# Right forms in quarter-size pieces, and pairs of two kinds in alternation, in the up-projection of a gated MLP

## The chip, the cores and the metric

The kernel runs on one core of a Trainium2 chip. The core has TensorE (PE, matrix products; its weight loads are listed as PEld), VectorE (DVE), ScalarE (ACT), GpSimd (POOL) and SyncE (SP, which here only issues DMAs). Each engine works through its own list of instructions in order, and engines wait for each other through semaphores. The metric is the device time of one execution in microseconds (us).

## The reference

One layer of a decoder trunk on a sequence of 1024 positions and 1024 channels: a block of three mixers, a cross-attention, and a gated MLP. The change lies in the gated MLP:

```
def conv_gated_ffn(h, w_up, conv_w, conv_b, w_down):
    u, v = jnp.split(h @ w_up, 2, axis=-1)
    u = causal depthwise convolution of width 3 (u, conv_w) + conv_b
    return (jax.nn.silu(u) * v) @ w_down
```

The block is cut here to its core. `h @ w_up` is 1024x1024 by 1024x5632, so u and v have 2816 channels each, which are 22 blocks of 128 (`NFF` = 22).

## The kernel before

`ffn_up` computes `h @ w_up` as 22 pairs. Pair f is the u block f and the v block 22 + f, 128 channels each, over all 1024 positions. The two halves of the positions and the two halves of the inner dimension make it a 2x2x2 block product, and it is done with seven products in place of eight (a Winograd form). Each product is a left form (made of weights) by a right form (made of activations).

A product (`prod`, L1292 to 1297) is 12 matmuls of 128x128 by 128x512: four steps of the inner dimension, and three for each, since every form is split into a rounded part `hi` and a rest `lo`, and hi·hi, hi·lo and lo·hi are summed. It needs the `lo` of its left form from the second or third matmul on, not at the first.

**Left forms** (`left`, L1263 to 1290). GpSimd makes the sums S1 to S4 of the weight blocks (L1280), ScalarE casts the hi part (L1287), and VectorE or GpSimd subtracts it for the lo part (L1288). In the kernel before, the forms take turns: one on VectorE, the next on GpSimd. A form lies in a tile `wf` from a pool with two tags of two buffers each, so a fifth form has to wait until TensorE has finished with the first.

**Right forms** (`right`, L1299 to 1319) are built once. From the transposed activations in four tiles `h3r` (128x2048) it makes T1 to T4 and takes B22 as it is; each is then split in hi (ScalarE, L1306) and lo (L1307; VectorE for T1 to T3, GpSimd for T4 and B22). Every step is one instruction of 128x2048.

**Work ahead** (`ahead`). While the activations are still being made and while the right forms are built, TensorE does the products A11·X0 and A12·X1 of pairs 0 to 7 (they need plain activations only), and the results go to DRAM (`part`) by way of `s1` (after the first product) and `c11` (L1353, after both, out of the bank `ps_a`). So pairs 0 to 7 have five products left, T2, T3, T1, T4, B22 in the code's order, and pairs 8 to 21 have seven, with A11 and A12. In the following they are called fives and sevens. A five holds 60 matmuls, a seven 84.

**A pair** (`pair`, L1355 to 1395) sums its products in PSUM: `ps_b2` for T2 (pool mps), `ps_cd` with two halves for T3+T4 and T1+B22 (pool dps, two buffers), `ps_a` for A11+A12. VectorE reads them out into u2, u3, vt and u (L1377 to 1388), and when u is complete the convolution and the gate follow: ScalarE L1390, VectorE L1391 and L1392, ScalarE's silu L1393, GpSimd's multiplication y·vt L1394 (128x1024), and a DMA to DRAM. The weights of the next pair are loaded when a pair is begun.

The pairs run in the order 0 to 21: eight fives, then fourteen sevens. `ffn_down` follows and reads y from DRAM (`acr`), splits it into `ap` (L1444, L1445) and multiplies (L1431, tile `ps_dn`).

Each engine's order of instructions is not the order of the code: a scheduler that simulates the program sets it when the kernel is built, so that products of neighbouring pairs are interleaved. A change of sizes or of the loop's order moves instructions on all engines.

Of the kernel before, what the change touches and what calls it, by code (L numbers as in the profile page):

```python
# [12 lines left out]
F32 = mybir.dt.float32  # L13
# [4 lines left out]
ALU = mybir.AluOpType  # L18
# [9 lines left out]
NFF = 22  # L28
# [68 lines left out]
class K:  # L97
# [1169 lines left out]
    def left(self, r1, r2, which, sp):  # L1267

        nc = self.nc
        V, A, G = nc.vector, nc.scalar, nc.gpsimd  # L1270
        q = {f"A{n}{k + 1}": r[:, 4 * k:4 * k + 4, :] for n, r in ((1, r1), (2, r2)) if r is not None for k in range(2)}
        sums = {"S1": ("A21", "A22", ALU.add), "S2": ("S1", "A11", ALU.subtract), "S3": ("A11", "A21", ALU.subtract),
                "S4": ("A12", "S2", ALU.subtract)}

        def get(n):
            if n not in q:
                a, b, op = sums[n]
                a, b = get(a), get(b)
                q[n] = b if n == "S4" else sp.tile([P, 4, P], F32, tag=n, name=n)
                G.tensor_tensor(out=q[n], in0=a, in1=b, op=op)  # L1280
            return q[n]

        for n in which:
            x = get(n)
            self.nform = getattr(self, "nform", 0) + 1
            f = self.wp.tile([P, 2, 4, P], F32R, tag=("whi", "wlo")[self.nform % 2], name="wf")
            A.copy(out=f[:, 0], in_=x)  # L1287
            (V if self.nform % 2 else G).tensor_tensor(out=f[:, 1], in0=x, in1=f[:, 0].bitcast(F32), op=ALU.subtract)  # L1288
            yield f

    def prod(self, ps, f, x, start, stop):
# [7 lines left out]
    def right(self, X, raw):  # L1299

        nc = self.nc
        V, A, G = nc.vector, nc.scalar, nc.gpsimd

        def parts(x, nm, eng):
            f = [self.quad(f"{nm}{p}") for p in ("hi", "lo")]
            A.copy(out=f[0], in_=x)  # L1306
            eng.tensor_tensor(out=f[1], in0=x, in1=f[0].bitcast(F32), op=ALU.subtract)  # L1307
            return f
        b11, b21, b12, b22 = raw[0, 0], raw[1, 0], raw[0, 1], raw[1, 1]
        V.tensor_tensor(out=b11, in0=b12, in1=b11, op=ALU.subtract)  # L1310
        t2 = self.quad("t2r", F32)
        V.tensor_tensor(out=t2, in0=b22, in1=b11, op=ALU.subtract)
        G.tensor_tensor(out=b12, in0=b22, in1=b12, op=ALU.subtract)
        X["T2"] = parts(t2, "T2", V)
        X["T3"] = parts(b12, "T3", V)
        G.tensor_tensor(out=b21, in0=b21, in1=t2, op=ALU.subtract)
        X["T1"] = parts(b11, "T1", V)
        X["T4"] = parts(b21, "T4", G)
        X["B22"] = parts(b22, "B22", G)

    def ffn_up(self, X, raw, act, part, spill):

        nc, tc, I = self.nc, self.tc, self.I
        V, A, G, T = nc.vector, nc.scalar, nc.gpsimd, nc.tensor
        with tc.tile_pool(name="up", bufs=1) as sp:
            col = lambda j, f: self.pc("ffn_conv_w", NFF * j + f) if j < 3 else self.pc("ffn_conv_b", f)
            nraw = itertools.count()
            ne = part.shape[1]

            def load(m):  # L1330
                n = next(nraw) % 6
                r = self.wp.tile([P, NK, P], F32, tag="raw", name="raw") if n < 2 else \
                    self.res.tile([P, NK, P], F32, tag=f"r{n}", name="raw")
                nc.sync.dma_start(out=r, in_=I["t_up"][m])
                return r
# [10 lines left out]
            def ahead(f):  # L1346
                forms, a = self.left(load(f), None, ("A11", "A12"), sp), bank(f)
                self.prod(a, next(forms), X[0], True, True)
                nc.sync.dma_start(out=part[0, f], in_=copy("s1", a))
                yield  # L1350
                self.prod(a, next(forms), X[1], False, True)
                c = spill.tile([P, 512], F32, tag="acr", name="c11")
                A.copy(out=c, in_=a)  # L1353
                nc.sync.dma_start(out=part[1, f], in_=c)
                yield  # L1355
# [42 lines left out]
            for f in range(ne):  # L1398
                g = ahead(f)
# [3 lines left out]
                prev = g  # L1403
            next(prev)
            self.right(X, raw)
            rs = [load(0), load(NFF)]
            for f in range(NFF):
                nx = [load(f + 1), load(NFF + f + 1)] if f + 1 < NFF else None
                pair(f, rs)
                rs = nx  # L1410

# [133 lines left out]
```

## Time and profile of the kernel before

| what | value |
|---|---|
| median of 3 runs | 2471.76 us (2469.12 to 2471.86) |
| the profiled execution | 2471.44 us, of which the trace spans 2469.7 us |
| TensorE busy | 2361.9 us, 96% of the span, 15224 matmuls |
| VectorE, ScalarE, GpSimd busy | 1256.0 us (51%), 884.7 us (36%), 758.3 us (31%) |
| mean granted clock of TensorE | 0.987 of full speed |
| ffn_up from the right forms to the end | about 1757 to 2228 us of the span |

Times within the trace are microseconds from the span's start. In a row of the timeline, the number in square brackets at its end is the idle time of the engine before this instruction and what ended it. A matmul's row shows 0.39 us, but the next one may start 0.23 us after it began, since matmuls overlap.

### The profile page before, as it was taken

How to read it: one execution, taken by the hardware profiler on the slowest of the kernel's cores; microseconds unless marked ns; L12 is line 12 of the kernel's file. 1: busy time of each engine (PE TensorE's matmuls, PEld its weight loads, DVE VectorE, ACT ScalarE, POOL GpSimd, SP SyncE). 2: the span in 40 equal slices, each digit the busy share in tenths (PEclk: the TensorE clock that was granted, in tenths of full speed). 3: DMA queues.
4: the chain of work that ended last, by engine and by line, in shares of the span. 5: the costliest groups of instructions: out<-in, count | busy, mean ns of one | idle time of the engine just before them, and what ended most of it. 6: DMA issues, size and time to landing. Idle time of an engine off the chain costs nothing. (4 is left out here: it accounts for less than half of the span.)

```text
span 2469.7 us, 37037 instructions
## 1 busy us (share of the span) xinstructions
PE 2361.9 (96%) x15224; PEld 1968.0 (80%) x15224; DVE 1256.0 (51%) x1964; ACT 884.7 (36%) x1359; POOL 758.3 (31%) x613
## 2 busy tenths in 40 slices
PE   7999999999999999999999999999898999999998
PEld 7987768686777887878787789999776777777887
DVE  6446465657336447463653554544645544466322
ACT  6543222231215335353541222433433333344321
POOL 1011011110112314233321620430577666764210
PEclk9999999999999999999999999999999999999999
DMA  8644213121222111111114541224453222237431
GB/s 301 233 153 128 82 57 95 57 95 40 95 68 68 59 46 35 52 43 52 43 65 166 180 162 35 94 77 138 132 174 130 91 80 77 77 113 272 158 135 47
DMA packets 100329, 259.45 MB, mean 105 GB/s; under 512 B 26048, under 2 KB 30784, under 8 KB 100160
## 3 DMA queue, kind: packets, MB, share of 16 engines
q1 hardware_dynamic: 98720, 253.01, 31.2%
q0 software_dynamic: 1008, 3.67, 0.5%
q8 instruction: 119, 1.95, 0.3%
q14 instruction: 50, 0.41, 0.0%
q10 hardware_dynamic: 432, 0.41, 0.0%
HBM read 195.19 MB, written 61.87 MB: 104 GB/s over the span
## 5 line engine op out<-in xcount | busy, mean ns | idle before, releaser
L155 PE MATMUL ps_d<-hThi,whi 128*128 128x512 f32 x1056 | 426.1, 404 | 2.1 <-DVE Ktt L261 1.7
L157 PE MATMUL ps_d<-hTlo,whi 128*128 128x512 f32 x1056 | 424.8, 403 | 0.0
L159 PE MATMUL ps_d<-hThi,wlo 128*128 128x512 f32 x1056 | 423.9, 402 | 0.0
L140 ACT CAST whi<-raw 128x1024 fp32r<-128x1024 f32 (+1 forms) x162 | 158.5, 985 | 339.3 <-PE ps_d L157 171.0
L1431 PE MATMUL ps_dn<-wd,ap 128*128 128x512 f32 x1056 | 242.3, 391 | 5.3 <-ACT ap L1444 3.0
L1431 PEld LDWEIGHTS ps_dn<-wd,ap 128*128 128x128 f32 x1056 | 199.1, 189 | 48.4 <-ACT ap L1444 3.9
L155 PEld LDWEIGHTS ps_d<-hThi,whi 128*128 128x128 f32 x1056 | 199.8, 189 | 44.7 <-issue 3.2
L157 PEld LDWEIGHTS ps_d<-hTlo,whi 128*128 128x128 f32 x1056 | 199.9, 189 | 43.0 <-issue 4.8
L159 PEld LDWEIGHTS ps_d<-hThi,wlo 128*128 128x128 f32 x1056 | 199.7, 189 | 42.7 <-issue 4.2
L143 POOL TENSOR_TENSOR wlo<-raw,whi 128x1024 fp32r<-128x1024 f32 (+1 forms) x45 | 96.0, 2133 | 446.1 <-ACT whi L140 353.9
L143 DVE TENSOR_TENSOR wlo<-raw,whi 128x1024 fp32r<-128x1024 f32 (+1 forms) x117 | 147.7, 1271 | 95.0 <-ACT whi L140 94.9
L1295 PE MATMUL ps_a<-h3hi,wf 128*128 128x512 f32 x352 | 118.0, 402 | 8.7 <-DVE wf L1288 6.7
L1287 ACT CAST wf<-S 128x512 fp32r<-128x512 f32 x88 | 54.7, 622 | 143.4 <-PE ps_cd L1295 96.9
L1445 DVE TENSOR_TENSOR ap<-acr,ap 128x512 fp32r<-128x512 f32 x44 | 44.2, 1006 | 114.6 <-ACT ap L1444 114.6
L1109 POOL TENSOR_SCALAR ms<-ms 128x1 f32<-128x1 f32 x33 | 8.3, 251 | 287.4 <-ACT xn L1108 178.4
L1295 PEld LDWEIGHTS ps_a<-h3hi,wf 128*128 128x128 f32 x352 | 67.6, 193 | 27.7 <-DVE wf L1288 8.0
L1442 POOL TENSOR_TENSOR wd<-wdr,wd 128x1024 fp32r<-128x1024 f32 x22 | 56.5, 2569 | 93.4 <-ACT wd L1441 84.9
L155 PE MATMUL ps_d<-ohi,whi 128*128 128x512 f32 x192 | 75.7, 398 | 7.2 <-ACT ohi L1160 7.2
L745 DVE CUSTOM_DVE_ANT_0 a_p<-ps_s,a_bias 128x512 f32<-128x512 f32 (+3 forms) x96 | 51.8, 553 | 52.4 <-PE ps_s L743 46.9
L1094 PE MATMUL ps_tm<-whi,h2Thi 128*128 128x256 f32 x256 | 75.3, 294 | 1.7 <-ACT s_p L1222 1.7
L755 ACT ACTIVATE a_p<-a_p,a_nm 128x128 f32<-128x128 f32 (+7 forms) x64 | 49.2, 769 | 76.4 <-POOL a_nm L751 59.5
L157 PE MATMUL ps_d<-olo,whi 128*128 128x512 f32 x192 | 76.1, 396 | 0.3 <-DVE olo L1161 0.3
(411 smaller groups left out, 5680.8 us busy)
## 6 DMA issues: line engine op xcount, KB each, us to landing
raw<-t_in SPq DMA_DIRECT2D x66, 512.0 KB, 3.8
raw<-t_up SPq DMA_DIRECT2D x52, 512.0 KB, 3.7
wdr<-ffn_w_down SPq DMA_DIRECT2D x44, 512.0 KB, 4.3
th_dram<-th SPq DMA_DIRECT2D x24, 512.0 KB, 2.8
mth<-th_dram SPq DMA_DIRECT2D x24, 512.0 KB, 3.7
acr<-act_dram SPq DMA_DIRECT2D x44, 256.0 KB, 2.7
act_dram<-y SPq DMA_DIRECT2D x20, 512.0 KB, 2.6
raw<-t_kv SPq DMA_DIRECT2D x16, 512.0 KB, 5.0
```

The lines of the kernel that those rows point to most:

```text
L140: nc.scalar.copy(out=hi, in_=raw)
L143: eng.tensor_tensor(out=lo, in0=raw, in1=hi.bitcast(F32), op=ALU.subtract)
L155: nc.tensor.matmul(o, lhsT=hi[:, k, :], rhs=xhi(k, h), start=(k == 0), stop=False)
L157: nc.tensor.matmul(o, lhsT=hi[:, k, :], rhs=xlo(k, h), start=False, stop=False)
L159: nc.tensor.matmul(o, lhsT=lo[:, k, :], rhs=xhi(k, h), start=False, stop=(k == nk - 1))
L745: V.tensor_tensor_reduce(out=p_[:, a:b], in0=ps[:, 0:b - a], in1=bias[:, 1024 - n + a:1024 - n + b], op0=ALU.add, op1=ALU.max, scale=1.0, ...
L755: A.activation(out=pr[c][:, 0:n], in_=pr[c][:, 0:n], func=AF.Exp, bias=nm[:, c:c + 1], accum_out=Z[:, c:c + 1])
L1094: nc.tensor.matmul(o, lhsT=xh, rhs=hi[:, k % 4, :], start=(k == 0), stop=False)
L1287: A.copy(out=f[:, 0], in_=x)
L1295: self.nc.tensor.matmul(ps, lhsT=f[:, a, k, :], rhs=x[b][:, k, :], start=(start and n == 0), stop=(stop and n == 11), skip_group_check=not ...
L1431: T.matmul(ps[j][c], lhsT=a[:, p, P * j:P * j + P], rhs=w[q][:, 512 * c:512 * c + 512], start=(f == 0 and n == 0), stop=(f == NFF - 1 and ...
L1442: (V if f % 2 else G).tensor_tensor(out=w[:, 1], in0=wr, in1=w[:, 0].bitcast(F32), op=ALU.subtract)
```

## The change

Three edits. In `right`, every instruction of 128x2048 becomes four of 128x512, one for each step k of the inner dimension; cast and lo alternate within a form in the code. In `left`, the lo parts go two to VectorE and one to GpSimd in turn, where they went one and one. In `ffn_up`, the loop takes the pairs in the order 0, 8, 1, 9, ... 7, 15, 16, ... 21: a five and a seven alternate eight times, then six sevens.

```
-            (V if self.nform % 2 else G).tensor_tensor(out=f[:, 1], in0=x, in1=f[:, 0].bitcast(F32), op=ALU.subtract)
+            (V if self.nform % 3 else G).tensor_tensor(out=f[:, 1], in0=x, in1=f[:, 0].bitcast(F32), op=ALU.subtract)
...
+        def sub(eng, out, in0, in1):
+            for k in range(4):
+                eng.tensor_tensor(out=out[:, k, :], in0=in0[:, k, :], in1=in1[:, k, :], op=ALU.subtract)
+
         def parts(x, nm, eng):
             f = [self.quad(f"{nm}{p}") for p in ("hi", "lo")]
-            A.copy(out=f[0], in_=x)
-            eng.tensor_tensor(out=f[1], in0=x, in1=f[0].bitcast(F32), op=ALU.subtract)
+            for k in range(4):
+                A.copy(out=f[0][:, k, :], in_=x[:, k, :])
+                eng.tensor_tensor(out=f[1][:, k, :], in0=x[:, k, :], in1=f[0][:, k, :].bitcast(F32), op=ALU.subtract)
             return f
...
-        V.tensor_tensor(out=b11, in0=b12, in1=b11, op=ALU.subtract)
+        sub(V, b11, b12, b11)
...
-        G.tensor_tensor(out=b21, in0=b21, in1=t2, op=ALU.subtract)
+        sub(G, b21, b21, t2)
...
+            order = [f for g in range(ne) for f in (g, ne + g)] + list(range(2 * ne, NFF))
             rs = [load(0), load(NFF)]
-            for f in range(NFF):
-                nx = [load(f + 1), load(NFF + f + 1)] if f + 1 < NFF else None
+            for n, f in enumerate(order):
+                nx = [load(order[n + 1]), load(NFF + order[n + 1])] if n + 1 < NFF else None
                 pair(f, rs)
                 rs = nx
```

The lines after these move down: the read-outs of a pair stand at L1382 to L1393 in the changed kernel, the matmul of `ffn_down` at L1437. The `sub` of the right forms is at L1306, the cast at L1311 and the lo at L1312.

Where the instructions stand is shown at three places. The first is the building of the right forms, on VectorE. `h3r00` is b11 in the code, `h3r01` is b12, and `wf_15720` is the left form A12 of one of the pairs that are done ahead; TensorE needs it next after `wf_15741`. Before:

```order
L1310 TENSOR_TENSOR h3r00_14875<-h3r01_15439,h3r00_14875 128x2048
L1312 TENSOR_TENSOR t2r_15913<-h3r11_15446,h3r00_14875 128x2048
L1307 TENSOR_TENSOR T2lo_15917<-t2r_15913,T2hi_15916 128x2048
L1307 TENSOR_TENSOR T3lo_15921<-h3r01_15439,T3hi_15920 128x2048
L1288 TENSOR_TENSOR wf_15720<-raw_15660,wf_15720 128x512
L1307 TENSOR_TENSOR T1lo_15926<-h3r00_14875,T1hi_15925 128x2048
L1288 TENSOR_TENSOR wf_15759<-raw_15699,wf_15759 128x512
```

and now:

```order
L1306 TENSOR_TENSOR h3r00_14875<-h3r01_15439,h3r00_14875 128x512 x4
L1306 TENSOR_TENSOR t2r_15916<-h3r11_15446,h3r00_14875 128x512 x4
L1288 TENSOR_TENSOR wf_15741<-raw_15738,wf_15741 128x512
L1312 TENSOR_TENSOR T2lo_15926<-t2r_15916,T2hi_15925 128x512 x4
L1312 TENSOR_TENSOR T3lo_15936<-h3r01_15439,T3hi_15935 128x512 x4
L1312 TENSOR_TENSOR T1lo_15950<-h3r00_14875,T1hi_15949 128x512 x4
L1288 TENSOR_TENSOR wf_15720<-raw_15660,wf_15720 128x512
L1288 TENSOR_TENSOR wf_15780<-raw_15777,wf_15780 128x512
```

T1lo stood behind the lo of `wf_15720`, and now its four pieces stand ahead of it; the lo of `wf_15741` came over from GpSimd. On ScalarE at the same place (`c11_15657` is the copy that frees the bank for TensorE's next product), before:

```order
L1306 CAST T2hi_15916<-t2r_15913 128x2048
L1306 CAST T3hi_15920<-h3r01_15439 128x2048
L1353 COPY c11_15657<-ps_a_15602 128x512
L1287 CAST wf_15720<-raw_15660 128x512
L1306 CAST T1hi_15925<-h3r00_14875 128x2048
```

and now:

```order
L1311 CAST T2hi_15925<-t2r_15916 128x512 x4
L1311 CAST T3hi_15935<-h3r01_15439 128x512 x4
L1311 CAST T1hi_15949<-h3r00_14875 128x512 x4
L1358 COPY c11_15657<-ps_a_15602 128x512
L1287 CAST wf_15720<-raw_15660 128x512
```

The four pieces of T1hi stand ahead of `c11_15657` now.

The second place is TensorE's order among pairs, here the first row of each product. Before, between two fives (`ps_cd_16168` and `ps_b2_16167` belong to one five, `ps_cd_16276` and `ps_b2_16275` to the next):

```order
L1295 MATMUL ps_cd_16060<-B22hi_15933,wf_16134 128x512
...
L1295 MATMUL ps_b2_16275<-T2hi_15916,wf_16283 128x512
...
L1295 MATMUL ps_cd_16168<-T1hi_15925,wf_16209 128x512
...
L1295 MATMUL ps_cd_16276<-T3hi_15920,wf_16301 128x512
...
L1295 MATMUL ps_cd_16168<-T4hi_15929,wf_16225 128x512
...
L1295 MATMUL ps_cd_16276<-T3hi_15920,wf_16301 128x512 x2
...
L1295 MATMUL ps_cd_16168<-B22hi_15933,wf_16242 128x512
...
L1295 MATMUL ps_b2_16383<-T2hi_15916,wf_16391 128x512
```

and now, one round of a five (`ps_cd_16488`, `ps_b2_16487`) and a seven (`ps_cd_16364`, then `ps_a_16589` and `ps_b2_16610` of the next seven):

```order
L1295 MATMUL ps_cd_16241<-B22hi_15969,wf_16315 128x512
...
L1295 MATMUL ps_cd_16488<-T3hi_15935,wf_16513 128x512
...
L1295 MATMUL ps_cd_16364<-T1hi_15949,wf_16405 128x512
...
L1295 MATMUL ps_b2_16487<-T2hi_15925,wf_16495 128x512
...
L1295 MATMUL ps_cd_16364<-T4hi_15959,wf_16437 128x512
...
L1295 MATMUL ps_cd_16364<-B22hi_15969,wf_16454 128x512
...
L1295 MATMUL ps_a_16589<-h3hi0_14873,wf_16590 128x512
...
L1295 MATMUL ps_cd_16488<-T1hi_15949,wf_16529 128x512
...
L1295 MATMUL ps_cd_16611<-T3hi_15935,wf_16636 128x512
...
L1295 MATMUL ps_b2_16610<-T2hi_15925,wf_16618 128x512
...
L1295 MATMUL ps_cd_16488<-T4hi_15959,wf_16545 128x512
```

The T3 of the next five now stands right behind the B22 of the five before it, T2 right behind the T1 of a seven, and A11 of the next seven right behind the B22 of a seven. Before, T2 stood right behind B22, and T3 right behind T1.

The third place is the end, where the last pair meets `ffn_down`. Before (first rows of each group):

```order
L1295 MATMUL ps_cd_18634<-T1hi_15925,wf_18675 128x512
L1431 MATMUL ps_dn_18753<-wd_18763,ap_18766 128x512 x2
...
L1431 MATMUL ps_dn_18753<-wd_18763,ap_18766 128x512 x4
...
L1431 MATMUL ps_dn_18758<-wd_18763,ap_18766 128x512 x3
L1431 MATMUL ps_dn_18753<-wd_18797,ap_18800 128x512 x2
...
L1431 MATMUL ps_dn_18758<-wd_18797,ap_18800 128x512
L1295 MATMUL ps_cd_18634<-T4hi_15929,wf_18707 128x512
...
L1431 MATMUL ps_dn_18753<-wd_18797,ap_18800 128x512 x4
```

and now:

```order
L1295 MATMUL ps_cd_18676<-T1hi_15949,wf_18717 128x512
L1437 MATMUL ps_dn_18795<-wd_18805,ap_18808 128x512 x2
L1437 MATMUL ps_dn_18797<-wd_18805,ap_18808 128x512
L1295 MATMUL ps_cd_18676<-T4hi_15959,wf_18749 128x512
...
L1437 MATMUL ps_dn_18797<-wd_18805,ap_18808 128x512
L1437 MATMUL ps_dn_18798<-wd_18805,ap_18808 128x512 x2
```

Before, 27 matmuls of `ffn_down` stood ahead of the last T4; now it is 3.

## Rows read from the trace of the kernel before

**Rows 1.** Windows of the four stretches: engines' busy us (instructions), clock, DMA share, GB/s

```profile
1757.50:1805.10 47.60, 40.34 (x156) 31.81 (x157) 33.24 (x12) 23.71 (x32) 38.78 (x13) 0.89 0.45 135
1805.10:1953.40 148.30, 133.60 (x553) 102.82 (x552) 74.42 (x82) 49.64 (x67) 96.76 (x74) 0.99 0.40 131
1953.40:2205.40 252.00, 250.12 (x1081) 200.84 (x1080) 115.51 (x135) 96.39 (x143) 168.25 (x120) 1.00 0.24 78
2205.40:2240.00 34.60, 29.29 (x118) 22.79 (x117) 26.49 (x18) 18.38 (x22) 22.87 (x12) 0.95 0.74 243
```

**Rows 2.** Timeline, TensorE, right forms

```profile
1764.24 0.39 PE L1295 MATMUL ps_a<-h3lo,wf 128*128 128x512 f32 x1
...
1766.96 0.39 PE L1295 MATMUL ps_a<-h3lo,wf 128*128 128x512 f32 x1
...
1769.14 0.50 PE L1295 MATMUL ps_a<-h3hi,wf 128*128 128x512 f32 x1 [0.43 <-ACT c L1353]
...
1777.09 1.22 PE L1295 MATMUL ps_a<-h3hi,wf 128*128 128x512 f32 x2 [4.08 <-DVE wf L1288]
...
1781.88 0.40 PE L1295 MATMUL ps_a<-h3lo,wf 128*128 128x512 f32 x1
...
1785.35 1.22 PE L1295 MATMUL ps_a<-h3hi,wf 128*128 128x512 f32 x2 [2.60 <-DVE wf L1288]
```

**Rows 3.** Timeline, VectorE, right forms: start us, us, engine, line, operation, idle before

```profile
1757.50 2.29 DVE L1310 TENSOR_TENSOR h3r<-h3r,h3r 128x2048 f32<-128x2048 f32 x1 [2.31 <-ACT h3r L1256]
...
1764.16 4.65 DVE L1307 TENSOR_TENSOR T2lo<-t2r,T2hi 128x2048 fp32r<-128x2048 f32 x1 [1.98 <-ACT T2hi L1306]
1768.73 3.37 DVE L1307 TENSOR_TENSOR T3lo<-h3r,T3hi 128x2048 fp32r<-128x2048 f32 x1
1772.03 5.01 DVE L1288 TENSOR_TENSOR wf<-raw,wf 128x512 fp32r<-128x512 f32 x1
```

**Rows 4.** Timeline, GpSimd, right forms

```profile
1759.93 6.73 POOL L1313 TENSOR_TENSOR h3r<-h3r,h3r 128x2048 f32<-128x2048 f32 x1 [2.44 <-DVE h3r L1310]
1766.61 3.34 POOL L1288 TENSOR_TENSOR wf<-raw,wf 128x512 fp32r<-128x512 f32 x1
1769.91 6.58 POOL L1316 TENSOR_TENSOR h3r<-h3r,t2r 128x2048 f32<-128x2048 f32 x1
```

**Rows 5.** Timeline, ScalarE, right forms

```profile
1762.22 1.91 ACT L1306 CAST T2hi<-t2r 128x2048 fp32r<-128x2048 f32 x1
...
1768.52 0.57 ACT L1353 COPY c<-ps_a 128x512 f32<-128x512 f32 x1
```

**Rows 6.** Timeline, all engines, between two five-product pairs

```profile
1844.36 0.69 DVE L1388 TENSOR_TENSOR u<-ps_cd,u 128x512 f32<-128x512 f32 x1 [3.45 <-PE ps_cd L1295]
1844.42 0.62 ACT L1287 CAST wf<-S 128x512 fp32r<-128x512 f32 x1 [2.11 <-PE ps_cd L1295]
...
1851.36 2.38 POOL L1394 TENSOR_TENSOR y<-y,vt 128x1024 f32<-128x1024 f32 x1
...
1852.48 1.80 DVE L1288 TENSOR_TENSOR wf<-S,wf 128x512 fp32r<-128x512 f32 x1
```

**Rows 7.** Timeline, TensorE, five-product pairs

```profile
1845.09 0.50 PE L1295 MATMUL ps_b<-T2hi,wf 128*128 128x512 f32 x1 [0.76 <-ACT wf L1287]
...
1852.43 0.50 PE L1295 MATMUL ps_cd<-T3hi,wf 128*128 128x512 f32 x1 [0.71 <-ACT wf L1287]
...
1861.65 0.50 PE L1295 MATMUL ps_b<-T2hi,wf 128*128 128x512 f32 x1 [0.76 <-ACT wf L1287]
...
1863.17 0.62 PE L1295 MATMUL ps_b<-T2hi,wf 128*128 128x512 f32 x2
```

**Rows 8.** Timeline, TensorE, the step from the last five to the first sevens

```profile
1949.01 0.73 PE L1295 MATMUL ps_cd<-T1hi,wf 128*128 128x512 f32 x1 [2.33 <-DVE u L1379]
```

**Rows 9.** Timeline, TensorE, last T1 product and the first products of ffn_down

```profile
2209.63 2.11 PE L1431 MATMUL ps_dn<-wd,ap 128*128 128x512 f32 x8 [1.34 <-ACT ap L1444]
2213.92 6.22 PE L1431 MATMUL ps_dn<-wd,ap 128*128 128x512 f32 x19 [2.18 <-DVE ap L1445]
```

More of the change, by code (lines that the diff above doesn't have):

```diff
@@ L1302, in right @@
         V, A, G = nc.vector, nc.scalar, nc.gpsimd
+        def sub(eng, out, in0, in1):
+            for k in range(4):
+                eng.tensor_tensor(out=out[:, k, :], in0=in0[:, k, :], in1=in1[:, k, :], op=ALU.subtract)
         def parts(x, nm, eng):
             f = [self.quad(f"{nm}{p}") for p in ("hi", "lo")]
-            A.copy(out=f[0], in_=x)
-            eng.tensor_tensor(out=f[1], in0=x, in1=f[0].bitcast(F32), op=ALU.subtract)
+            for k in range(4):
+                A.copy(out=f[0][:, k, :], in_=x[:, k, :])
+                eng.tensor_tensor(out=f[1][:, k, :], in0=x[:, k, :], in1=f[0][:, k, :].bitcast(F32), op=ALU.subtract)
             return f
         b11, b21, b12, b22 = raw[0, 0], raw[1, 0], raw[0, 1], raw[1, 1]
-        V.tensor_tensor(out=b11, in0=b12, in1=b11, op=ALU.subtract)
+        sub(V, b11, b12, b11)
         t2 = self.quad("t2r", F32)
-        V.tensor_tensor(out=t2, in0=b22, in1=b11, op=ALU.subtract)
-        G.tensor_tensor(out=b12, in0=b22, in1=b12, op=ALU.subtract)
+        sub(V, t2, b22, b11)
+        sub(G, b12, b22, b12)
         X["T2"] = parts(t2, "T2", V)
         X["T3"] = parts(b12, "T3", V)
-        G.tensor_tensor(out=b21, in0=b21, in1=t2, op=ALU.subtract)
+        sub(G, b21, b21, t2)
         X["T1"] = parts(b11, "T1", V)
```

## The prediction

> **What bounds the kernel now.** I read the windows of the up-projection first [rows 1], then the timeline of each engine in the stage before the first pair's T2, then TensorE's waits in the fives, then the end. An unhindered product shows the pace: from 1764.24 to 1766.96, 12 matmuls take 2.72 us, 0.227 each [rows 2]. By that pace the windows say what is lost in each stretch. While the right forms are built, 156 matmuls need 35.4 of 47.6 us: 12.2 lost. In the fives and the step to the sevens, 553 (552 by the page's weight loads) need 125.3 of 148.3: 23.0 lost. In the sevens, 13 pairs of 84 matmuls would need 247.9 of 252.0; some records are missing there, and by the 1081 shown it is 6.6 lost, which I take, 0.5 a pair. At the end 118 need 26.8 of 34.6: 7.8 lost. The change can touch about 50 us, and each loss is a wait of TensorE for a form that is late, not a lack of capacity: VectorE is busy in 33.2 of the 47.6 us and in half of the rest, GpSimd in 38.8 and in two thirds.
>
> **The right forms: what holds them.** TensorE waits 0.43 us for a copy at 1769.14, 4.08 for a lo of VectorE up to 1777.09, and 2.60 for another up to 1785.35 [rows 2]. After the wait of 4.08 the granted clock is low for a while: 11 matmuls take 4.79 us (1777.09 to 1781.88) where 2.50 would do, 2.3 lost; the stretch's mean clock is 0.89 [rows 1], between the full level of 2.4 GHz and the lower of 1.2.
>
> Why is a lo of 128x512 late, listed with 5.01 us [rows 3]? VectorE and GpSimd take turns, whole instruction by whole instruction. An undisturbed 128x2048 on VectorE takes 2.29 (1757.50). T2lo is listed with 4.65: it ends at 1768.81, 2.15 after GpSimd's instruction has ended at 1766.66 [rows 4]. GpSimd's lo of 128x512 then ends at 1769.95, 1.14 behind T2lo; T3lo at 1772.10, 2.15 behind that; GpSimd's next 128x2048 at 1776.49, 4.39 behind T3lo; the late lo at 1777.04, 0.55 behind that. So a quarter costs VectorE 0.55 and GpSimd 1.10 to 1.14, one after the other, and TensorE's lo has to wait its turn.
>
> The Trainium skill (SBUF — State Buffer, Who interferes with whom) states this as a rule: a VectorE instruction with two SBUF inputs and a GpSimd one that reads SBUF exclude each other, and the loser "fully blocks". The rows above agree with it (the five ends that follow each other). By that rule pieces cannot shorten the sum of both engines' times, only what one small instruction waits for a single turn: the sum below stands. But the same section lets whoever starts first have the ports and speaks of no turns; if VectorE got them again between its own pieces, its list would run at its undisturbed pace, which is the first rival.
>
> **Edit 1, the pieces.** Five VectorE instructions, four GpSimd ones and five casts become four each: 42 more instructions. The cast of a whole form takes 1.91 [rows 5] and that of a quarter-sized left form 0.62 [rows 6], so four take up to 2.48: 0.6 more a form. A VectorE piece takes 0.69 undisturbed (the 128x512 read-out in [rows 6], the nearest row; bound below 2.29/4 = 0.57), four 2.76 against 2.29. None of this lies on TensorE; what counts is when the lo of `wf_15720` is done, since TensorE stands for it. In the new order VectorE has 22 pieces up to and with that lo (b11, t2, T2lo, T3lo, T1lo four each, two lo's), and GpSimd 13 in that time (b12, b21, T4lo four each, one lo). In turns: 22 × 0.55 + 13 × 1.14 = 26.9 us after 1757.50, thus 1784.4; laid out piece by piece with the casts between, I get 1784.9. Before it was 1777.04, since T1lo stood behind it and GpSimd had been given only two long turns. The copy of `c11`, at 1768.52 before [rows 5], stands behind the casts of t2, whose pieces now alternate with b21's, and behind T1hi: 1774.0 by the same layout, so TensorE already stands still from 1768.7 to 1774, then does one product and stands again up to 1785.0. From there to the T2 of pair 0 it has 94 matmuls: 11 at the slow pace (4.79) and 83 × 0.227 = 18.8, so T2 starts at 1808.6, where it was 1805.1. **Term A: +3.5.** The later wait of 2.60 is inside this and gone, since by then the lo's behind it had time. Bounds: if pieces let the lo through as soon as its cast is there, all waits of the stretch but about 1.6 vanish, −10.6; if the wait of 2.60 comes as well, with a slow stretch of 1.6 behind it, +7.7. I take the value of the layout, which rests on the five ends above.
>
> **Edit 2, two lo's of three on VectorE.** It takes some 26 lo's from GpSimd (of 154). Undisturbed one is 0.69 on VectorE. In the pairs neither is the bound, and by the turns above a lo costs the other engine its turn anyway: nothing, with the bounds inside term B.
>
> **Edit 3, the alternation.** First what a five loses. From 1845.09 to 1861.65 a five takes 16.56 where 60 matmuls need 13.62 [rows 7]: 2.9 lost. The waits: T2's form gets its buffer only when the product right before it (B22) ends, then the cast follows (1844.42, 0.62 [rows 6]); an idle time of 0.76 by the row, 0.92 by the pace (a matmul's row of 0.39 hides 0.16). T2 then waits for its lo: from 1861.65 to 1863.17 five matmuls take 1.52 against 1.14, 0.39 lost, and a little more where GpSimd makes it. T3 waits in the same way (0.71, so 0.87) behind T1. The step to the sevens costs once more, with 2.33 at 1949.01 and a slow clock behind it [rows 8].
>
> In the new order every five and seven together have these places. T3 of the next five right behind the B22 of the one before: `ps_cd` has two buffers, so it waits for VectorE's read-out, which ended at 1845.05 where B22's last matmul began at 1843.94 (the read-out in [rows 6] starts 1844.36 and takes 0.69): 0.95. T2 of the five right behind a seven's T1, its form in T1's buffer: 0.92 and its lo. That lo is on VectorE at the time when GpSimd multiplies y·vt of the five before. Such a meeting is in the trace: the multiplication runs from 1851.36 to 1853.74, and the lo of VectorE that came at 1852.48 is listed with 1.80, 1.11 more than 0.69 [rows 6]. So the lo costs 0.39 if they miss each other and 1.50 if they meet so; I take 1.32, as in my layout the multiplication starts 0.2 sooner. A11 of the next seven right behind a seven's B22: 0.92 + 0.39 = 1.31. Sum: 0.95 + 2.24 + 1.31 = 4.50 a round.
>
> Over the stretch: 6 × 0.95 = 5.7, 6 × 2.24 = 13.4, 7 × 1.31 = 9.2; the first A11 0.9, the second five's T2 0.7; at the last A11, where the round ends, 3.1 with the clock (1.3 without it; the nearest row is the 2.33 in [rows 8]); six sevens × 0.5 = 3.0. Together 36.0, against 23.0 + 6.6 = 29.6 before. **Term B: +6.4.** If the multiplication is missed and the last one is 1.3, it is 36.0 − 6 × 0.93 − 1.8 = 28.6, −1.0. If the alternation spares TensorE all waits of the kind, only the sevens' loss stays, 22 × 0.5 = 11: −18.6. What speaks against that: the waits behind the product just before are two in a five before, and two in a round now.
>
> **The end.** TensorE waits 1.34 and 2.18 for `ap` of `ffn_down` [rows 9]. Now only 3 of its matmuls stand ahead of T4, and T4's 2.72 us lie where the 2.18 was. The read-outs behind T4 are early then, and what follows is the same. **Term C: −1.5**, with bounds 0 and −2.2.
>
> **Sum.** 3.5 + 6.4 − 1.5 = +8.4 on the profiled execution of 2471.4 us, of which 2469.7 are the trace: 2479.8. The median of the runs is 0.3 above that execution; I leave it out.
>
> **The rivals.** One: *the pieces let the small lo's through*. If a piece on either engine gives way after 0.55 or 1.14 us, and the casts come early, the lo's that TensorE needs are done before it asks for them, and A is −10.6, B −1.0, C −1.5: 2458.3. 22 pieces at 0.69 would end at 1772.7, before the c11 copy of the layout; it decides if `wf_15720` is there before 1774. For it: single turns are short. Against: the five ends in turn above, and the engines' lists are fixed: T1lo now stands ahead of the lo. Two: *the waits only change places*. A is about 0, as the stage has the same work for both engines, the multiplication misses the lo's, B −1.0, C −1.5: 2468.9, within 0.2% of now. For it: every wait lost before has one of its kind in the new order. Against: the layout. Three: *worse by a step*. The second wait stays (A +7.7) and the sevens in the rounds lose as much as the fives, one wait of 0.9 more in each of 8: B +13.6; with C, 2491. Four: *the alternation frees TensorE*: B −18.6, with A +3.5 and C, 2454.8; nothing in the trace shows such a pair. That the pairs would not alternate on TensorE at all is excluded by the order.
>
> **How the numbers follow.** Chances: forecast 0.45, one 0.15, two 0.27, three 0.06, four 0.07. A difference of 0.2%, 4.9 us, is about what a measurement of this kernel can tell from none. The forecast's own range, from its bounds (−1.0 or +6.4 in B, A some 3 around), is 2470 to 2485. For the whole, with cases of both signs, 2458 leaves out case four and part of one, and 2487 case three. Slower by over 0.2%: most of the forecast (0.41) and case three, 0.47. Faster: one, four, and a bit of two, 0.24. Same: 0.29.
>
> **What would show it.** In the trace of the changed kernel: the T2 of pair 0 starts 47 us behind the first subtraction before, and 51 by A; a wait of TensorE for the copy of c11 of some 5 us and one for a lo of VectorE of about 8 follow each other. VectorE's lo there are listed with 1.7 us each in place of 0.69, in turns with GpSimd's. In the rounds T3 waits for a read-out of VectorE (0.8 by the row), T2 for a cast and a lo, A11 for a cast, some 4.5 in 32.7 us of matmuls. The prediction is wrong if TensorE passes `wf_15720` without a long wait, if a round takes less than 36 us, or if the y·vt multiplication and the lo of T2 never meet.

## The result, and the profile after

The changed kernel takes 2493.19 us (median of 6 runs, 2489.65 to 2496.60) against 2471.81 for the kernel before: the ratio is 1.0079, with a 95% interval of 1.0063 to 1.0095, so 16 to 23 us slower. The forecast was slower by 8 us. The profiled execution spans 2491.9 us, 22.2 more than before, and the difference is in three pieces. The first T2 starts at 1802.06, 3.1 us earlier than before. From there to the last matmul of the last pair's T1 it takes 430.8 us where it took 402.8: 28.0 more. From there to the end it is 2.8 less.

The windows of the changed kernel, cut at the same events as [rows 1] (right forms; rounds of five and seven; the last sevens; the end). The columns are those of [rows 1]:

```profile
1757.70:1802.06 44.36, 38.16 (x156) 30.48 (x157) 28.90 (x28) 25.05 (x47) 38.60 (x25) 0.92 0.40 129
1802.06:2111.00 308.94, 278.52 (x1153) 216.06 (x1151) 149.78 (x171) 104.54 (x146) 166.38 (x128) 0.98 0.31 101
2111.00:2232.90 121.90, 117.06 (x492) 93.45 (x492) 62.84 (x69) 43.34 (x63) 63.54 (x45) 0.97 0.22 71
2232.90:2270.00 37.10, 33.88 (x141) 27.31 (x140) 30.68 (x19) 19.37 (x24) 23.81 (x11) 0.95 0.78 267
```

In the rounds TensorE is busy in 278.5 of 308.9 us, at a granted clock of 0.98. What it waits for, over all pairs, is in the view of the waits (engine and tile that waits, what it waits for, us in total, times, the longest). Before:

```profile
PE ps_b L1295 <- ACT wf L1287: 6.6, 13, 0.8
PE ps_cd L1295 <- ACT wf L1287: 4.4, 6, 0.9
PE ps_cd L1295 <- DVE u L1379: 2.3, 1, 2.3
PE ps_b L1295 <- POOL wf L1288: 1.9, 3, 0.6
PE ps_a L1295 <- ACT wf L1287: 0.7, 1, 0.7
```

and after:

```profile
PE ps_b L1295 <- DVE wf L1288: 9.6, 9, 1.3
PE ps_a L1295 <- ACT wf L1287: 7.5, 9, 1.8
PE ps_cd L1295 <- DVE vt L1391: 5.5, 7, 0.8
PE ps_cd L1295 <- DVE u L1393: 5.3, 6, 0.9
PE ps_b L1295 <- ACT wf L1287: 4.5, 7, 0.7
PE ps_a L1295 <- DVE wf L1288: 2.0, 1, 2.0
```

By kind: waits for casts of forms (`ACT wf`) were 12 us and still are. New are waits for lo's of VectorE (`DVE wf`, 11.6 us), and waits for read-outs (`DVE vt`, `DVE u`) have grown from one of 2.3 to 10.8 us in 13. In all it is 35 us of waits against 16. The other 9.3 of the 28.0 us are in TensorE's busy time, which rises from 386.2 to 395.6: a matmul that starts after a wait is listed longer, and the clock falls in some rounds. One round, TensorE's rows that waited or ran slow:

```profile
1868.16 0.47 PE L1295 MATMUL ps_cd<-T3hi,wf 128*128 128x512 f32 x1 [0.88 <-DVE u L1393]
...
1874.58 0.50 PE L1295 MATMUL ps_b<-T2hi,wf 128*128 128x512 f32 x1 [0.71 <-ACT wf L1287]
...
1876.37 0.73 PE L1295 MATMUL ps_b<-T2hi,wf 128*128 128x512 f32 x2 [1.06 <-DVE wf L1288]
...
1878.28 1.05 PE L1295 MATMUL ps_b<-T2hi,wf 128*128 128x512 f32 x2
...
1884.05 0.50 PE L1295 MATMUL ps_cd<-B22hi,wf 128*128 128x512 f32 x1 [0.79 <-DVE vt L1391]
...
1887.82 0.50 PE L1295 MATMUL ps_a<-h3hi,wf 128*128 128x512 f32 x1 [0.71 <-ACT wf L1287]
```

T3 of the next five waits for a read-out, T2 for its cast and then for its lo. Two matmuls take 1.05 us at 1878.28 where 0.62 is listed elsewhere: the granted clock is at its lower level, 1.2 GHz, after the two waits. Then comes a wait for which the forecast had no term: B22 of the seven at 1884.05, right behind its own pair's T4, stands 0.79 us for VectorE's read-out L1391. Then A11 at 1887.82 for its cast. The read-outs, and the lo of T2 with GpSimd's y·vt beside it, in the timeline of all engines:

```profile
1867.33 0.69 DVE L1393 TENSOR_TENSOR u<-ps_cd,u 128x512 f32<-128x512 f32 x1 [4.09 <-PE ps_cd L1295]
...
1873.41 2.36 POOL L1399 TENSOR_TENSOR y<-y,vt 128x1024 f32<-128x1024 f32 x1 [0.97 <-ACT y L1398]
...
1874.56 1.76 DVE L1288 TENSOR_TENSOR wf<-S,wf 128x512 fp32r<-128x512 f32 x1 [1.70 <-ACT wf L1287]
...
1883.31 0.69 DVE L1391 TENSOR_TENSOR vt<-ps_cd,u 128x512 f32<-128x512 f32 x1 [1.73 <-PE ps_cd L1295]
```

L1391 at 1883.31 reads the half c, into which T4 went. B22 goes into the half d. It waits until that read has ended at 1884.00 all the same. T3 at 1868.16 is the same case the other way round: it goes into a half c and waits for L1393, which reads a half d.

The right forms in the timeline of VectorE (compare [rows 3]; x4 are four pieces in one row):

```profile
1762.34 6.88 DVE L1306 TENSOR_TENSOR t2r<-h3r,h3r 128x512 f32<-128x512 f32 x4
1769.14 1.76 DVE L1288 TENSOR_TENSOR wf<-raw,wf 128x512 fp32r<-128x512 f32 x1
1770.82 3.56 DVE L1312 TENSOR_TENSOR T2lo<-t2r,T2hi 128x512 fp32r<-128x512 f32 x4
1774.30 2.49 DVE L1312 TENSOR_TENSOR T3lo<-h3r,T3hi 128x512 fp32r<-128x512 f32 x4
1776.71 2.48 DVE L1312 TENSOR_TENSOR T1lo<-h3r,T1hi 128x512 fp32r<-128x512 f32 x4
1779.12 1.28 DVE L1288 TENSOR_TENSOR wf<-raw,wf 128x512 fp32r<-128x512 f32 x2
```

of GpSimd (compare [rows 4]):

```profile
1765.23 6.79 POOL L1306 TENSOR_TENSOR h3r<-h3r,t2r 128x512 f32<-128x512 f32 x4
1776.11 5.45 POOL L1288 TENSOR_TENSOR wf<-raw,wf 128x512 fp32r<-128x512 f32 x1 [4.09 <-ACT wf L1287]
```

and of ScalarE (compare [rows 5]):

```profile
1773.93 0.58 ACT L1358 COPY c<-ps_a 128x512 f32<-128x512 f32 x1
```

The pieces of t2 take 1.7 us each, in turns with GpSimd's subtractions (6.79 for the four of b21), as forecast, and so does the lo at 1769.14 (1.76). From 1772.02, where b21 ends, to 1776.11 GpSimd has nothing ready, since its next lo waits for a cast. T3lo and T1lo run at 0.62 a piece, and so do the lo's behind them, and that does not change when GpSimd's lo is ready at 1776.11: the four pieces of T1lo and two lo's, all of which start later, go ahead of it, and it ends at 1781.56, 1.16 behind the last of them (1780.40). It got no turn between them. So the lo of `wf_15720`, the first of the two at 1779.12, is done at about 1779.8, 5 us sooner than the layout had it. TensorE's one long wait there is the one for the copy of `c11` (TensorE's timeline, that wait and the first T2):

```profile
1774.56 0.80 PE L1295 MATMUL ps_a<-h3hi,wf 128*128 128x512 f32 x1 [5.63 <-ACT c L1358]
...
1802.06 0.39 PE L1295 MATMUL ps_b<-T2hi,wf 128*128 128x512 f32 x1
```

That copy ran at 1773.93, where the forecast had 1774.0.

TensorE's timeline at the step out of the rounds into the last sevens (compare [rows 8]):

```profile
2111.04 0.50 PE L1295 MATMUL ps_a<-h3hi,wf 128*128 128x512 f32 x1 [1.79 <-ACT wf L1287]
...
2113.76 1.22 PE L1295 MATMUL ps_a<-h3hi,wf 128*128 128x512 f32 x2 [1.99 <-DVE wf L1288]
```

and at the end (compare [rows 9]):

```profile
2235.78 1.65 PE L1437 MATMUL ps_dn<-wd,ap 128*128 128x512 f32 x3 [2.53 <-ACT ap L1450]
2237.23 0.63 PE L1295 MATMUL ps_cd<-T4hi,wf 128*128 128x512 f32 x1
```

### The profile page after: what moved, and what is told of

Same layout as the page of the kernel before. It is cut to its first block, busy times and chain, and to the rows that moved or that the text cites. A ratio compares the mean times of both kernels' runs of the same rounds, so it can differ in the third digit from the quotient of the medians.

```text
span 2491.9 us, 37049 instructions
## 1 busy us (share of the span) xinstructions
PE 2369.3 (95%) x15224; PEld 1972.1 (79%) x15224; DVE 1270.0 (51%) x2005; ACT 887.7 (36%) x1374; POOL 717.9 (29%) x599
## 4 chain that ended last, share of the span: by engine, by line
PE 71%; DVE 11%; issue 8%; ACT 4%; DMA 3%; POOL 3%; SPq 0%; DVEq 0%; POOLq 0%; ACTq 0%
PE ps_d L157 9%; PE ps_d L159 9%; PE ps_d L155 9%; PE ps_cd L1295 9%; PE ps_dn L1437 6%; PE ps_a L1295 3%; PE ps_tm L1094 3%; PE ps_tm L1095 3%; PE ps_tm L1096 3%; PE ps_b L1295 2%; PE ps_l L942 1%; PE ps_c L279 1%; DVE tmpa L453 1%; DVE tha L455 1%; PE ps_Y L279 1%
## 5 line engine op out<-in xcount | busy, mean ns | idle before, releaser
L1437 PE MATMUL ps_dn<-wd,ap 128*128 128x512 f32 x1056 | 241.0, 390 | 3.2 <-ACT ap L1450 3.2
L1437 PEld LDWEIGHTS ps_dn<-wd,ap 128*128 128x128 f32 x1056 | 198.5, 188 | 45.1 <-ACT ap L1450 4.1
L1451 DVE TENSOR_TENSOR ap<-acr,ap 128x512 fp32r<-128x512 f32 x44 | 37.4, 856 | 114.6 <-ACT ap L1450 114.6
L1288 DVE TENSOR_TENSOR wf<-S,wf 128x512 fp32r<-128x512 f32 x56 | 53.2, 949 | 73.2 <-ACT wf L1287 70.8
L1280 POOL TENSOR_TENSOR S<-raw 128x512 f32<-128x512 f32 x44 | 57.7, 1312 | 69.7 <-DVE wf L1288 68.3
L1295 PE MATMUL ps_b<-T2hi,wf 128*128 128x512 f32 x176 | 63.3, 422 | 14.4 <-DVE wf L1288 9.6
```

What stands on the lines that cost most here:

```text
L1295: self.nc.tensor.matmul(ps, lhsT=f[:, a, k, :], rhs=x[b][:, k, :], start=(start and n == 0), stop=(stop and n == 11), skip_group_check=not ...
L1437: T.matmul(ps[j][c], lhsT=a[:, p, P * j:P * j + P], rhs=w[q][:, 512 * c:512 * c + 512], start=(f == 0 and n == 0), stop=(f == NFF - 1 and ...
```

## The experiments

Two theories were to be told apart at first. One: the alternation is the loss, and in it the waits for read-outs, since the two halves of `ps_cd` are one tile and a product waits for the latest read of it, whichever half that was. The other: the loss is in the lo's moved to VectorE, or in the pieces. Times are medians, each with its ratio to the kernel before on the same chip; not all runs were on one chip, so small differences between two of them are read from the ratios. Where the traces of two runs are compared and a few matmuls of the work ahead fall on the other side of the first T2, they are counted off at 0.227 us each.

**Only the right forms in pieces** (the loop and `nform % 2` as before). 

> Only the right forms in quarters; the lo's go one and one and the pairs run 0 to 21 as before. Theory: the pieces earn some 3 us, since VectorE keeps its turns between its own pieces and the first T2 starts at about 1802 in place of 1805.1, and nothing else of the change is in it: 2467 to 2470. Rival (the one on record): the pieces alternate with GpSimd's, the lo of wf_15720 comes late and the first T2 at 1808: 2474 to 2476.

Measured: 2471.55 us, 0.9998 (0.9988 to 1.0007): no difference that can be told, and neither range. From the first subtraction to the first T2 it takes some 1.8 us less than before by the traces, but TensorE waits the same 5.63 us for the copy of `c11` as in the changed kernel, and the casts and lo's that wait in the fives are as in [rows 7]. A gain of 3 us is at the edge of the interval; a loss of 3.5, the prediction's term, is outside it.

**Only the alternation** (the loop of the change, nothing else).

> Only the order of the pairs (0, 8, 1, 9, ...), with whole right forms and lo's one and one. Theory: the alternation is the whole loss; in its order on TensorE the B22 of a seven again stands right behind its T4, T3 of the next five right behind a B22, A11 behind a B22, so a round loses 5 to 7 us in place of some 3.4, and the time is 2490 to 2500. Rival: the lo's that were moved to VectorE make T2 late (1.2 us a round and the slow clock behind it), and without them a round loses 4: 2476 to 2483.

Measured: 2510.66, 1.0145 (1.0126 to 1.0164). The alternation alone costs more than the whole change; the theory had the direction, and its range was left by 10 us. The rival fell: without the moved lo's it is worse, not better. The waits of TensorE over all pairs, columns as above:

```profile
PE ps_b L1295 <- DVE wf L1288: 8.8, 7, 1.3
PE ps_b L1295 <- ACT wf L1287: 7.8, 8, 1.2
...
PE ps_cd L1295 <- DVE vt L1386: 5.5, 7, 0.8
PE ps_cd L1295 <- DVE u L1388: 5.3, 6, 0.9
PE ps_a L1295 <- POOL wf L1288: 4.4, 7, 0.6
```

The read-outs cost the same as in the changed kernel (5.5 and 5.3 us, 13 times). Added are 4.4 us for lo's of GpSimd, which are A11's, and longer waits for T2's casts (7.8 in place of 4.5).

**Only the lo's, two to VectorE and one to GpSimd** (`nform % 3`).

> Only the lo's, two to VectorE and one to GpSimd in turn. Theory: in the fives and sevens in their old order neither engine is the bound; 2468 to 2474 (the end has T4 behind 3 matmuls of ffn_down here, some 2 us less). Rival: a lo on VectorE that meets y·vt on GpSimd costs 1.2 us in each five: 8 x 1.2 and more, 2480 and above.

Measured: 2470.04, 0.9987 (0.9978 to 0.9995), the time that the theory gave, but by luck. Against the kernel before, the trace has some 3.5 us less up to the first T2 and 3.0 us less at the end (3 matmuls of `ffn_down` ahead of the last T4 in place of 27), and some 4.5 us more in the pairs. There TensorE's waits grow from 16 to 21 us, with a kind that the kernel before did not have:

```profile
PE ps_b L1295 <- DVE wf L1288: 5.8, 5, 1.3
```

So the edit is not without effect on the pairs; its parts cancel.

**The alternation with one of the two other edits each.** TensorE's order within the rounds is the same in these two, in the alternation alone and in the changed kernel, so there they differ only in who makes the lo's; the stage before, some of the last sevens and the end are in another order too.

> The alternation with the lo's two to one, right forms whole. TensorE's order in the rounds is the same as with the alternation alone and as in the changed kernel. Theory: the lo's are what takes some 15 of the 18 us between these two (A11's lo comes from VectorE, 0.16 lost in place of 0.80, T2's cast waits 0.7 in place of 1.2), the pieces some 3: 2494 to 2498. Rival: the pieces take most of it: 2503 to 2512.

Measured: 2490.02, 1.0081 (1.0066 to 1.0096).

> The alternation with right forms in pieces, lo's one and one; the counterpart of the run before. Theory: 2504 to 2510 (the alternation alone less some 3). Rival: 2493 to 2498.

Measured: 2503.46, 1.0132 (1.0112 to 1.0151). So the lo's take 0.0064 of the ratio off the alternation's 0.0145, some 16 us, as the theory said; both runs came out somewhat lower than expected, the first by 4 us. The pieces' 0.0013, some 3 us, is inside the intervals, and beside the lo's they earn nothing that can be told (1.0079 with them, 1.0081 without).

**Two tiles in place of one.** The change as it is, but the halves are tiles of their own, here and in `ffn_down`:

```
-                cd = self.dps.tile([P, 1024], F32, tag="d", name="ps_cd")
-                c, d = cd[:, 0:512], cd[:, 512:1024]
+                c, d = (self.dps.tile([P, 512], F32, tag=t, name=f"ps_{t}") for t in "cd")
...
+    b.pst.close()
+    b.dps = ctx.enter_context(tc.tile_pool(name="cds", bufs=2, space=PSUM))
+    b.tps = ctx.enter_context(tc.tile_pool(name="tpu", bufs=2, space=PSUM))
```

> The changed kernel with the two halves of ps_cd as two PSUM tiles of 512 (ps_c, ps_d, two buffers each, the same space), also in ffn_down; everything else is the same, but the scheduler orders anew. Theory: B22 (half d) waits for VectorE's read-out of half c at L1391 only because both halves are one tile; with two tiles the waits of 1.05 at B22 and of 1.03 at T3 go in 7 and 6 rounds, with part of the slow clock: 14 to 20 us less than the changed kernel, 2473 to 2480. Rival: the read-out is needed for something else, or another wait (a form's cast) takes its place: within 4 us of the changed kernel, 2489 to 2497.

Measured: 2433.49, 0.9838 (0.9823 to 0.9853): 60 us less than the changed kernel and 39 less than the kernel before. The theory had the direction, and a quarter to a third of the size. The window from the first T2 to the end of the pairs:

```profile
1800.10:2178.00 377.90, 377.90 (x1669) 312.98 (x1667) 247.52 (x243) 150.62 (x213) 240.24 (x175) 1.00 0.35 111
```

and in TensorE's timeline the last matmul of a T4 and the first of the B22 behind it:

```profile
1897.84 0.39 PE L1296 MATMUL ps_c<-T4hi,wf 128*128 128x512 f32 x1
1898.06 0.39 PE L1296 MATMUL ps_d<-B22hi,wf 128*128 128x512 f32 x1
```

The B22 starts 0.22 us after T4's last matmul. TensorE is busy for 377.9 of 377.9 us, at full clock. Not only are the waits for read-outs gone, those for casts and lo's are too. TensorE's order is another here: with nothing to wait for between T3, T1, T4 and B22, the scheduler keeps the products nearly in the order of the code.

**Two tiles in the other kernels.**

> The kernel before with ps_c and ps_d as two tiles, nothing else of the change. Theory: the common tile costs twice, by its own waits (T1 for the read of T3's half, B22 for that of T4's) and since the scheduler, which knows these waits, puts products of the next pair in between, out of the order in which their forms got their buffers, so that later forms wait for a buffer; without it most of the 23 us of the fives go: 2446 to 2456. Rival: in the old order the scheduler had filled these places, so only the one wait of 2.49 at T1 and its slow clock go: 2465 to 2470.

Measured: 2441.64, 0.9867 (0.9850 to 0.9883): the theory's direction, 4 us below its range; the rival fell.

> Two tiles, right forms in quarters, lo's two to one, but the pairs 0 to 21: the run with two tiles less the alternation. Theory: with the waits of the common tile gone the order of the pairs is worth little: 2430 to 2440. Rival: the alternation earns by itself once the tile is out of the way, since a five needs a form for each 2.7 us with more sums than a seven: 2445 to 2455.

Measured: 2432.12, 0.9827 (0.9812 to 0.9841), as the theory said.

> Two tiles (ps_c, ps_d) and the alternation, right forms whole, lo's one and one: the run with the alternation alone but for the tile. Theory: the tile is behind nearly all of the alternation's cost; it comes to within 6 us of the kernel before with two tiles (2441.6): 2436 to 2448, where with one tile it was 2510. Rival: lo's one and one are late in the alternation in any case: 2452 to 2465.

Measured: 2438.44, 0.9871 (0.9857 to 0.9886), as the theory said. With two tiles the alternation is worth nothing that can be told, with the other two edits (0.9838 against 0.9827) or without them (0.9871 against 0.9867). With one tile it costs 38 us by itself. The other two edits together earn some 10 us with two tiles (0.9867 to 0.9827): by the traces 4.5 us before the first T2 and 3.4 in the pairs. With one tile they were run together in the alternation only, where they earn 16 (1.0145 to 1.0079).

**One tile, and two read-outs moved in the code.** No tile or buffer is another here:

```
-                V.tensor_tensor(out=u3, in0=c, in1=u2, op=ALU.add)
                 self.prod(d, next(forms), X["T1"], True, True)
+                V.tensor_tensor(out=u3, in0=c, in1=u2, op=ALU.add)
...
-                V.tensor_tensor(out=vt[:, 0:512], in0=c, in1=u2, op=ALU.add)
                 self.prod(d, next(forms), X["B22"], False, True)
+                V.tensor_tensor(out=vt[:, 0:512], in0=c, in1=u2, op=ALU.add)
```

> The changed kernel with one tile, but two read-outs later in the code: that of T3's half behind T1, that of T4's half behind B22. Nothing is added or left out. Theory: the wait is for the latest read of the tile that stands ahead in the code, whichever half it reads; T1 and B22 then wait for none, the scheduler has nothing to fill, and the time comes near that of two tiles: 2435 to 2455. Rival: two tiles helped by freeing each half's buffer sooner, which this does not: 2480 to 2495.

Measured: 2445.00, 0.9878 (0.9864 to 0.9893): 48 us less than the changed kernel, from the place of two lines and the order that the scheduler made with them. A B22 that stands right behind the T4 of its pair does not wait here, with one tile and a read of half c that comes later than in the changed kernel:

```profile
1872.06 0.39 PE L1295 MATMUL ps_cd<-T4hi,wf 128*128 128x512 f32 x1
1872.29 0.39 PE L1295 MATMUL ps_cd<-B22hi,wf 128*128 128x512 f32 x1
```

So the wait hangs on where the read stands in the code, and not on which half it reads or on how soon a half is free. The waits of TensorE over all pairs:

```profile
PE ps_b L1295 <- DVE wf L1288: 9.3, 7, 1.3
PE ps_cd L1295 <- DVE vt L1386: 2.3, 1, 2.3
```

Left are T2's lo of VectorE, seven times, and one read-out.

**A fifth buffer for the left forms.** The fifth lies in `sp`; `s1` has two buffers for three, `spill` three for four.

```
+            n = self.nform % 5
+            f = (sp if n == 4 else self.wp).tile([P, 2, 4, P], F32R, tag=("whi", "wlo", "whi", "wlo", "wf5")[n], name="wf")
```

> The changed kernel with five buffers for the left forms in place of four (room from s1, two in place of three buffers, and spill, three in place of four); one tile as before. Theory: a form waits for its buffer since products run out of the order of their forms; with a fifth the cast waits at T2 and A11 (0.87 and 1.25 in 7 rounds, with some slow clock) go and those for read-outs stay: 2465 to 2482. Rival: with the common tile the scheduler's order takes up the fifth as well: 2487 to 2497.

Measured: 2489.12, 1.0058 (1.0043 to 1.0073), near the changed kernel. The rival held by its time. The scheduler made another order with it: up to the last T1 the waits for casts fell from 12.0 to 5.0 us, those for read-outs rose from 11.3 to 15.4, and 5.6 us of waits for `ap` of `ffn_down` came among the pairs. So the run doesn't show what a fifth buffer would do in the same order. That forms wait because products run out of the order in which the forms got their buffers is thus not shown by it.

**The copy of c11 on VectorE**, on top of the best version:

> The best so far (two tiles, pieces, lo's two to one, pairs 0 to 21) with the copy of c11 on VectorE in place of ScalarE, so that it does not stand behind the twelve casts of T2, T3 and T1. Theory: TensorE's wait of 6.3 for that copy is set by ScalarE's order; 4 to 7 us go: 2425 to 2429. Rival: VectorE's pieces, in turns with GpSimd's, are as late, or the lo of wf behind it takes the wait over: 2430 to 2435.

Measured: 2434.77, 0.9859 (0.9843 to 0.9876), against 0.9827 (0.9812 to 0.9841) without: not faster, and by the ratios 0.3% slower, with intervals that just miss each other; the two runs were on different chips. TensorE has one wait there of 8.07 us in place of 6.3, now for VectorE's copy, which stands behind pieces of the lo's. The rival held. The trace shows something more at this copy:

```profile
1770.35 1.57 POOL L1289 TENSOR_TENSOR wf<-raw,wf 128x512 fp32r<-128x512 f32 x1 [3.12 <-ACT wf L1288]
1770.72 0.68 DVE L1359 COPY c<-ps_a 128x512 f32<-128x512 f32 x1
1771.32 1.76 DVE L1313 TENSOR_TENSOR T3lo<-h3r,T3hi 128x512 fp32r<-128x512 f32 x2
```

GpSimd's lo, which was held up for 5.45 us in the changed kernel, comes at 1770.35 in the middle of VectorE's pieces here, and ends at 1771.92. VectorE's next instruction was the copy, which has one input, in PSUM; the piece behind it had to wait instead.

## Why the prediction was wrong

The direction and the place were right: slower, by the alternation, with T3 behind a B22, T2 behind a T1 and A11 behind a B22 as the places where TensorE stands. The size was 8.4 where the trace shows 22.2 us. By its terms:

**Term A, +3.5, measured −3.1.** The step that failed is the count in strict turns, 22 × 0.55 + 13 × 1.14. It held for t2 against b21, and the copy of c11 came within 0.1 us of the layout. It did not hold once VectorE had pieces ready one behind the other and GpSimd came with a single lo: they ran at 0.62 and that lo was listed with 5.45 us, so TensorE passed `wf_15720` without a long wait, one of the signs that the prediction had named. The five ends in turn [rows 3, 4] were of both engines at work without a gap, and I carried their rule over to a stretch where one of them was not. The first rival had named this. It also said that its waits would then be gone; the wait for c11 stayed (5.63), so it was a gain of 3 us and not of 10. Nor is the gain the worth of the pieces: by the traces the lo's edit alone, with whole right forms, gains some 3.5 us up to the first T2, and the pieces alone some 1.8.

As the Trainium skill (SBUF — State Buffer, Who interferes with whom) has it, the loser fully blocks; the row of 5.45 agrees with that. The section also gives the ports to whoever issues first, for one instruction, and there this trace differs: six VectorE instructions that start from 1776.71 on went ahead of a GpSimd one that starts at 1776.11. Why the pieces of t2 did alternate and these did not isn't settled. It is not that each b21 piece needs a t2 piece: the lo at 1769.14 waited its turn as well (1.76), and no piece of b21 needs it.

**Term B, +6.4, measured +28.0.** The sum of a round was 4.50; the round from A11 at 1847.68 to A11 at 1887.82 takes 40.14 us for 144 matmuls, which need 32.7: 7.4 lost, in others 5.8, on the mean of six rounds 6.7. Of its places, three were right by their rows: T3 0.88 (with the 0.16 that a row hides, 1.04 against 0.95), T2 0.71 and 1.06 (2.3 by the pace against 2.24; its lo meets y·vt as forecast, listed with 1.76), A11 0.71 (1.25 against 1.31). What was left out is B22 behind T4: I took the halves of `ps_cd` as free of each other, though the row of 2.33 at a T1 that waits for `DVE u L1379` [rows 8] is such a wait, T1 in half d for the read of half c, and I priced it without asking what it was. B22's wait is 0.79, 0.95 by the pace, in 7 rounds. Nor did I count the clock that falls behind T2's two waits in every other round (about 1.6 us; 0.51 is the granted clock from 1877.30 to 1880.20), nor the full price of the step out of the rounds (1.79, 1.99 and a slow clock behind them, against the 3.1 I had taken). The estimate of the sevens at the end, 0.5 each, was low as well, with T2's lo late twice more.

Of the 21.6 us that the term fell short, by the pace, the six rounds make some 13 (B22 5.7 and the clock 4.8 of them), the stretch up to the first of them, the step out and the sevens some 3 each. The base of the sum was right, though not for the reason given: no records are missing in the sevens of the kernel before, and 1081 matmuls are what lies between the two times of the window; all 1848 of `ffn_up` are in the trace.

**Term C, −1.5, measured −2.8.** The mechanism was right: T4 stands behind three matmuls of `ffn_down`, and the wait of 2.18 in [rows 9] is gone; the first one grew from 1.34 to 2.53, and a later one for `ap` fell from 1.70 to 0.68. But the place of T4 comes with the lo's edit: with the other two edits alone it stands behind 27 as before.

**Edit 2, at nothing.** Wrong within the alternation, where it earned 16 us (1.0145 to 1.0081): by the two traces some 10 in the pairs, 4 before the first T2 and 4.6 at the end. Without it A11's lo had to come from GpSimd, at 0.6 us of waiting each time. By itself it earned 0.13%, since what it costs in the pairs of the old order takes most of its gain.

The rivals: the third, *worse by a step*, came nearest in time (2491), in part by luck. One half of it came true: the sevens in the rounds did lose one wait of 0.95 more each, B22's, in 7 of them, though it did not say where. The other half did not: the second wait of the first stage was gone, and the two misses, A too high and B too low, nearly cancel. The fourth, that the alternation frees TensorE, did not come true in any run: with two tiles almost nothing waits in the pairs, in either order.

What stays open is how the 60 us between one tile and two divide. They are what TensorE lost in the pairs of the changed kernel (57.6 by the pace), and with two tiles nothing is lost there. The 13 waits for read-outs make 10.8 us by the view of the waits, and 12.9 with 0.16 hidden in each; the rest came with the scheduler's other order, in which casts and lo's are early. A kernel with two tiles in the changed kernel's own order, which would tell the one from the other, was not tried.

## What to carry to other kernels

Before pricing a new order, look at each wait in the old one for what it protects: a product that waits for the read of the other half of its tile is a dependency of the code's making, and a reordering may expose it at more places. Giving the halves tiles of their own was worth 1.3% on the kernel before and 2.4% on the changed one, and putting the reads behind both products in the code 2.0% on the changed one; the alternation, which cost 1.45% with one tile, cost nothing that could be told with two. An edit whose time comes out as nothing may still hold a gain and a loss, so its trace is to be read stage by stage. Where two engines share a path, a rule of turns taken from a stretch where both are at work without a gap should not be carried to one where one of them is not, without a row that shows it.

## What the runs showed of the hardware

VectorE and GpSimd alternate, whole instruction by whole instruction, when both have subtractions in SBUF to do without a gap: 128x2048 [rows 3, 4], and 128x512 too (t2's pieces 1.7 us each beside b12's and b21's). But a row of VectorE's 128x512 pieces, one ready behind the other at 0.62 us, kept a GpSimd instruction that came by itself and takes 1.3 us alone busy for 5.45 (5.44 to 5.45 in the two kernels with two tiles and both other edits, and in the one with the read-outs moved). A VectorE copy out of PSUM in such a row let it in: 1.57.
